# Row sums of a softmax taken off TensorE: additions on GpSimd and VectorE in place of a column of ones, in a hybrid attention step on one NeuronCore

## The chip, the cores and the metric

One core of one Trainium2 chip runs the whole program. The metric is the device time of one execution in microseconds. The profile is one more execution of the same program, taken by the hardware profiler; its own time is 710.37 us.

## The reference, cut to what matters

One layer of a diffusion backbone: 1024 latent tokens and 128 prompt tokens, width 1024, all in float32. A combined projection feeds two groups of heads, mixer A (every latent token sees 128 cached and 1024 latent keys) and mixer B (a window of 128 each way, the cached keys and a sink logit). Both have 8 query heads and 2 key heads of 64. Their gated outputs go through one output projection. Mixer A for a block of 128 queries:

```python
def one_block(qblk):
    s = jnp.einsum('bqkgd,bskd->bkgqs', qblk, k_all).astype(jnp.float32) * (d ** -0.5)
    p = jax.nn.softmax(s, axis=-1).astype(v_all.dtype)
    return jnp.einsum('bkgqs,bskd->bqkgd', p, v_all)
...
def merge_out(o_a, g_a, o_b, g_b, w_out):
    return jnp.concatenate([o_a * jax.nn.silu(g_a), o_b * jax.nn.silu(g_b)], axis=-1) @ w_out
```

The change is about the softmax's denominator in mixer A and about how the values are multiplied.

## The kernel before, in words

To keep float32 accuracy, every operand of a product is split into a high part in TensorE's fp32r type and a low part, the rest. A product is then three: high by high, low by high, high by low. The first 300 us make the projections and are not touched.

After that the kernel works through units. A unit (t, m, g) is one block of 128 tokens t, one mixer m (0 is A, 1 is B) and one key head g, that is four query heads of 128 queries, 512 columns. The order is A, B, A, B for each of the eight latent blocks, so units with even numbers from 0 to 30 are A and odd ones B; then come four short units for the prompt. A latent A unit has nine blocks of 128 keys, a B unit four (three at the two ends). Each block is one *slot* of a written-out schedule (lines 1287 to 1344): in slot s the program issues the scores of block s, the work that is due in that slot (`due`, `later(n, f)`: n slots later), some output products (`outq`, at `OUTRATE` 2.5 a slot), and the products with the values of block s - 3 (`LAG`). Each engine executes its instructions in exactly this order (`in_order`), so an instruction that waits holds up all that stand behind it on its engine.

A block of A (function `scores`): TensorE makes `st` (keys by queries, lines 1179 and 1180; the second product adds minus the row maximum, which lies in rows 64 to 67 of `qb`), ScalarE makes `pe` = exp (L1182) and its high part `ph` (L1186), GpSimd the low part `pl` = pe - ph (L1190; block 4 is VectorE's, L1188). Three slots later `values` adds three products to the bank `pv`: `v_hi` by `ph` (L1200), `v_lo` by `ph` (L1202, 64 columns wide), `v_hi` by `pl` (L1203). For A, `v_hi` holds the values' high part beside 64 columns of ones, so rows 64 to 127 of `pv` are the softmax's row sums, already spread over 64 rows. At a unit's end (`END_AT`) ScalarE makes the sums' inverse by Ln and Exp (L1214, L1215), VectorE multiplies (L1224), GpSimd multiplies by the gate `sgl` (L1226), and the result is split into `ogh` and `ogl` (L1236, L1238) for the output products (L1271).

A B unit has its weights made ahead, while the A unit before it runs: TensorE makes `sn` (L994, L995), VectorE adds the mask and takes the maximum into `nm` (L998), ScalarE makes the exponentials `pen` (L984). Its four slots then only transpose `pen` (L1174), take the high part (L1175) and the low part (VectorE, L1176). B's row sums come as a by-product of L984; they are turned, written to DRAM and read back as rows spread over partitions (L1046 to L1057), and GpSimd multiplies `sgl` by them (L1042).

The next A unit's row maxima are made over A and B slots: products `pmx` (L939), VectorE's maxima `mx` (L940), `m_nat` (L949), a transpose `ptm` (L956) and `qb` (VectorE, L957).

PSUM has eight banks: two called A (pmx, sn, ptm, pti and others), two B (st), two C (pv), D and E (output products).

Of the kernel before, what the change touches and what calls it, by code (L numbers as in the profile page):

```python
# [34 lines left out]
KS = (0, 1, 4, 5, 2, 3, 6, 7)  # L35
PL_DVE = (4,)
LAG = 3
# [9 lines left out]
PH_DVE = 0  # L47
MX_NEXT = (-8, -7, -6, -5, -4, 4, 5, 5, 7, 7, 8, 8)
# [24 lines left out]
NOG = 5  # L73
PES = 3
GATE_LATE = 2
END_AT = (1, 4, 6, 9)
EDGE_END = (1, 3, 6, 9)
PROMPT_END = (2, 4, 5, 7)
# [40 lines left out]
def hybrid_step(ctx, tc, x_prompt, x_sample, cache_k_a, cache_v_a, cache_k_b, cache_v_b,  # L119
# [11 lines left out]
    gate_row = dram.tile([2, D], F32, name="gate_row")  # L131
    r_dram = [dram.tile([4, P], F32, name=f"rd{i}") for i in range(2 * NL)]

# [3 lines left out]
    def later(n, f):  # L137

        agenda.setdefault(now[0] + n, []).append(f)
# [625 lines left out]
    v_hi = kv.tile([P, 2, 20, 2, HD], F32R, name="v_hi")  # L765
    v_lo = kv.tile([P, 20, HD], F32R, name="v_lo")

# [6 lines left out]
    def split_values(src, j):  # L774

        nc.vector.tensor_tensor(v_lo[:, j : j + 2, :], src[:, 0], v_hi[:, 0, j : j + 2, 0, :], op=ALU.subtract)
        nc.vector.tensor_tensor(v_hi[:, 1, j : j + 2, 1, :], src[:, 1], v_hi[:, 1, j : j + 2, 0, :], op=ALU.subtract)

    with tc.tile_pool(name="kt", bufs=2) as kt:
        W_GB.pools[WRAW : WRAW + 2] = [(kt, 2)] * 2  # L780
        sg_tile.append(lambda n: kt.tile([P, 512], F32, tag="kh", name=n))
        for b in range(0, 20, 4):
            later(4 + b // 2, lambda b=b: nc.gpsimd.tensor_scalar(
                v_hi[:, 0, b : b + 4, 1, :], gain4, 0.0, 1.0, op0=ALU.mult, op1=ALU.add))
        ones = ident_r.bitcast(F32)[64:68].unsqueeze(1)
# [116 lines left out]
    qs = ctx.enter_context(tc.tile_pool(name="qs", bufs=2, side="right"))  # L902
    qs.tile([P, 32], F32, name="pad2", bufs=1)
    qp = ctx.enter_context(tc.tile_pool(name="qp", bufs=2, side="right"))
# [17 lines left out]
    def max_items(i):  # L922
# [4 lines left out]
        def item(h, b):  # L927
            if h == 0 and b == 0:
                mxtile[i] = qs.tile([P, 4, 3], F32, tag="mx", name=f"mx{i}", bufs=3)
            mx = mxtile[i]  # L930
            lhs = qtile[i][:, P * h : P * h + P]
            pm = bank("DE"[(h + b) % 2] if i in WIDE_MAX else "A", f"pmx{i}_{h}_{b}")
            if t == 0:
                for h in range(4):
                    hs = slice(P * h, P * h + P)
                    nc.tensor.matmul(pm[:, hs], qtile[i][:, hs], khp[:, g, :], start=True, stop=True)
                nc.vector.tensor_reduce(mx[:, :, 0], pm.rearrange("p (h n) -> p h n", h=4), axis=AX.X, op=ALU.max)
            else:
                nc.tensor.matmul(pm[:, 0:384], lhs, kha[:, g, 3 * b : 3 * b + 3, :], start=True, stop=True)  # L939
                nc.vector.tensor_reduce(mx[:, h, b : b + 1], pm[:, 0:384], axis=AX.X, op=ALU.max)  # L940
# [25 lines left out]
    def weight_items(i):  # L966
# [81 lines left out]
        def put():  # L1048
            iv = spare[0:4, 512 : 512 + P]
            (nc.vector.tensor_copy if i == 1 else nc.scalar.copy)(iv, v["pt"])  # L1050
            nc.sync.dma_start(r_dram[i // 2], iv)

        def rows():
            v["rows"] = spare[:, 512:768].rearrange("p (c n) -> p c n", c=2)
            for s in range(2):
                nc.sync.dma_start(v["rows"][HD * s : HD * s + HD],
                                  r_dram[i // 2].rearrange("(c s) n -> s c n", s=2)[s : s + 1].to_broadcast([HD, 2, P]))  # L1057

# [81 lines left out]
    def blocks(t, m, g):  # L1140

        if t == 0:
            k = (khp[:, g, :], klp[0:68, g, :]) if m == 0 else 0
            return [(k, v_hi[:, m, 18 + g], v_lo[:, 18 + g, :])]
        if m == 0:
            return [((kha[:, g, b, :], kla[:, g, b, :]), v_hi[:, 0, 2 * b + g], v_lo[:, 2 * b + g, :]) for b in range(9)]
# [19 lines left out]
    def scores(i, b, blk):  # L1166
# [13 lines left out]
        nc.tensor.matmul(s, kl, qbtile[i], start=False, stop=True)  # L1180
        pe = w3.tile([P, 512], F32, tag="pe", name=f"pe{i}_{b}", bufs=PES)
        nc.scalar.activation(pe, s, AF.Exp)  # L1182
        if i == 0 and b < PH_DVE:
            nc.vector.tensor_copy(ph, pe)
        else:
            nc.scalar.copy(ph, pe)  # L1186
        if b in PL_DVE:
            later(1, lambda: nc.vector.tensor_tensor(pl, pe, ph, op=ALU.subtract))  # L1188
        else:
            nc.gpsimd.tensor_tensor(pl, pe, ph, op=ALU.subtract)  # L1190
        return ph, pl

    def values(i, b, last, blk, ph, pl):
# [6 lines left out]
        nc.tensor.matmul(pv, two, ph, start=(b == 0), stop=False)  # L1200
        if m == 0:
            nc.tensor.matmul(pv[0:64, :], vl, ph, start=False, stop=False)  # L1202
# [6 lines left out]
        def inverse():  # L1209
            v["rs"] = w2.tile([64, 512], F32, tag="rs", name=f"rs{i}", bufs=1)  # L1210
            if m == 1:
                nc.scalar.copy(v["rs"], pv[64:128, :])
                return
            nc.scalar.activation(v["rs"], pv[64:128, :], AF.Ln)  # L1214
            nc.scalar.activation(v["rs"], v["rs"], AF.Exp, scale=-1.0)  # L1215

        def gated():
# [5 lines left out]
            for s in range(2):  # L1223
                nc.vector.tensor_tensor(of[64 * s : 64 * s + 64], pvv[:, :, s, :], srv[:, :, s, :],  # L1224
                                        op=ALU.add if m else ALU.mult)
            nc.gpsimd.tensor_tensor(of, of, sgl.pop(i), op=ALU.mult)  # L1226
            later(GATE_LATE, lambda: load_gate(i + 2))
            v["of"] = of

        def parts():  # L1230
            while held[0] == NOG:
                outq.pop(0)()
            held[0] += 1
# [5 lines left out]

        ends = (EDGE_END if m == 0 and t in (1, NL) else END_AT) if t else PROMPT_END  # L1240
        for n, f in zip(ends, (inverse, gated, parts)):
# [16 lines left out]
    def out_items(t, g):  # L1258
# [3 lines left out]
        def mm(n, k, p):  # L1262

            if k == KS[0] and p == 0:
                po[n] = bank("DE"[n], f"po{t}_{n}")
            if n == 0 and k == KS[4] and p == 0:
# [8 lines left out]
            if k == KS[-1] and p == 2:  # L1275
# [6 lines left out]

        ks = KS[4 * g : 4 * g + 4]
        return [lambda n=n, k=k, p=p: mm(n, k, p)
                for kk in ((ks[:2], ks[2:]) if last else (ks,)) for n in range(2) for k in kk for p in range(3)]
# [38 lines left out]
    for s in range(len(slots) + LAG + PROMPT_END[3]):  # L1324
# [83 lines left out]
```

## Time and profile before

| what | before |
|---|---|
| runs | 709.97, 710.36, 710.41 us, median 710.36 |
| profiled execution, its own time | 710.37 us |
| its span | 708.4 us |
| instructions | 10641 |
| mean clock of TensorE granted | 0.999 |
| busy PE / DVE / ACT / POOL | 98% / 63% / 59% / 47% of the span |

PE is TensorE's products, PEld its weight loads, DVE VectorE, ACT ScalarE, POOL GpSimd, SP the queue that issues most transfers. A group's row gives line, engine, operation, output and input tiles, shape and count, then busy us and mean ns of one, then the idle time in front of it and what ended it. A row of the timeline gives start and duration in us, then the same names. Matmuls overlap, so a matmul's cost is the distance from its start to the next one's, not its duration.

### The profile page before, as it was taken

The page shows a single profiled execution, that of the slowest core. Times are in us where ns is not written, and L with a number is a line of the kernel's source. Part 1 is how long each engine was busy: PE and PEld are TensorE (multiplying, and loading weights), DVE is VectorE, ACT ScalarE, POOL GpSimd, SP SyncE. Part 2 cuts the span into 40 slices and gives each one's busy share as a digit, 9 for nine tenths or more (in the row PEclk, how much of TensorE's full clock was granted, in tenths as well). Part 3 has the DMA queues.
Part 4 walks back from the last instruction along what each step waited for, and adds up shares of the span by engine and source line. Part 5 has one row for each costly group of instructions (what it writes and reads, how often), then busy time and mean ns, then how long its engine had stood idle before and what let it go on. Part 6 is the DMA issues. An engine that isn't in the chain of part 4 may idle for free.

```text
span 708.4 us, 10641 instructions
## 1 busy us (share of the span) xinstructions
PE 694.0 (98%) x3522; PEld 556.9 (79%) x3522; DVE 446.5 (63%) x995; ACT 414.6 (59%) x834; POOL 334.1 (47%) x349
## 2 busy tenths in 40 slices
PE   6999999999999999999999999999999999999997
PEld 2778988877788889976788788878888888787875
DVE  4555247866677763566667577567676775775563
ACT  5546412421324441179877877787788778877860
POOL 2456024233223330245877655755575547555751
PEclk9999999999999999999999999999999999999999
DMA  9951281238233026423222122122221221212323
GB/s 348 420 186 61 105 303 75 91 113 276 103 134 119 5 72 186 141 70 95 64 93 82 34 82 73 47 81 62 82 70 42 68 89 45 83 52 90 91 75 126
DMA packets 53303, 78.57 MB, mean 111 GB/s; under 512 B 6584, under 2 KB 25464, under 8 KB 52352
## 3 DMA queue, kind: packets, MB, share of 16 engines
q1 hardware_dynamic: 45936, 66.92, 28.9%
q10 hardware_dynamic: 7312, 10.98, 4.1%
q8 instruction: 28, 0.46, 0.3%
q14 instruction: 27, 0.22, 0.1%
HBM read 58.69 MB, written 19.18 MB: 110 GB/s over the span
## 4 chain that ended last, share of the span: by engine, by line
PE 92%; DMA 3%; ACT 2%; issue 1%; DVE 1%; POOL 1%; SPq 0%; ACTq 0%; POOLq 0%; DVEq 0%
PE po L1271 14%; PE pv L1203 7%; PE pv L1200 6%; PE st L1179 5%; PE pmx L939 5%; PE pq L262 5%; PE pq L264 5%; PE pq L263 5%; PE st L1180 5%; PE pv L1202 5%; PE st L1174 4%; PE pg L276 3%; PE pg L272 3%; PE pg L277 3%; PE pk L264 2%; PE pk L262 2%
## 5 line engine op out<-in xcount | busy, mean ns | idle before, releaser
L1190 POOL TENSOR_TENSOR pl<-pe,ph 128x512 fp32r<-128x512 f32 x130 | 167.7, 1292 | 151.2 <-ACT ph L1186 65.7
L940 DVE TENSOR_REDUCE mx<-pmx 128x1 f32<-128x384 f32 x192 | 100.9, 553 | 63.4 <-PE pmx L939 60.9
L1182 ACT ACTIVATE pe<-st 128x512 f32<-128x512 f32 x146 | 86.9, 595 | 29.6 <-PE st L1180 28.9
L1186 ACT CAST ph<-pe 128x512 fp32r<-128x512 f32 x146 | 90.6, 620 | 4.9
L1203 PE MATMUL pv<-pl,v_hi 128*128 128x512 f32 x208 | 82.5, 397 | 0.9 <-POOL pl L1190 0.5
L1200 PE MATMUL pv<-ph,v_hi 128*128 128x512 f32 x208 | 82.4, 396 | 0.0
L1271 PE MATMUL po<-wo,ogh 128*128 128x512 f32 x216 | 73.2, 395 | 0.1
L187 POOL TENSOR_TENSOR rs_q<-ms_q,mhalf 128x8 f32<-128x8 f32 x18 | 34.8, 1933 | 80.9 <-DVE ms_q L185 80.9
L998 DVE CUSTOM_DVE_ANT_0 sn<-sn,mask,nsink 128x512 f32<-128x512 f32 (+1 forms) x64 | 46.4, 725 | 39.1 <-PE sn L995 38.4
L939 PE MATMUL pmx<-kha,qt 128*128 128x384 f32 x192 | 60.4, 364 | 0.9 <-DVE nm L998 0.7
L1179 PE MATMUL st<-qt,kha 128*128 128x512 f32 x144 | 58.1, 403 | 0.7 <-DVE inv L1033 0.5
L1202 PE MATMUL pv<-ph,v_lo 128*64 128x512 f32 x146 | 57.6, 395 | 0.0
L1180 PE MATMUL st<-qb,kla 68*128 68x512 f32 x144 | 57.2, 398 | 0.0
L1203 PEld LDWEIGHTS pv<-pl,v_hi 128*128 128x128 f32 x208 | 39.2, 188 | 18.2 <-POOL pl L1190 1.0
L705 ACT CAST qo0q<-ptq 128x512 fp32r<-128x512 f32 x18 | 10.6, 587 | 65.8 <-PE ptq L702 65.3
L984 ACT ACTIVATE pen<-sn,nm 128x512 f32<-128x512 f32 (+2 forms) x72 | 45.0, 626 | 5.9 <-DVE nm L1011 2.6
L1175 ACT CAST ph<-st 128x512 fp32r<-128x512 f32 x62 | 36.4, 587 | 20.1 <-PE st L1174 18.8
L1271 PEld LDWEIGHTS po<-wo,ogh 128*128 128x128 f32 x216 | 39.9, 188 | 6.8 <-ACT ogh L1236 0.5
L1200 PEld LDWEIGHTS pv<-ph,v_hi 128*128 128x128 f32 x208 | 39.3, 189 | 6.7 <-ACT ph L1175 0.2
L1176 DVE TENSOR_TENSOR pl<-st,ph 128x512 fp32r<-128x512 f32 x62 | 42.6, 689 | 2.8 <-ACT ph L1175 2.2
L1271 PE MATMUL po<-wo,ogl 128*128 128x512 f32 x108 | 42.7, 395 | 0.3 <-POOL ogl L1238 0.3
L939 PEld LDWEIGHTS pmx<-kha,qt 128*128 128x128 f32 x192 | 35.2, 190 | 8.5 <-DVE mx L940 2.9
(230 smaller groups left out, 1687.4 us busy)
## 6 DMA issues: line engine op xcount, KB each, us to landing
qt<-qd SPq DMA_DIRECT2D x72, 128.0 KB, 2.9
wm<-in_w_mod_ss_dram SPq DMA_DIRECT2D x7, 1024.0 KB, 9.4
qd<-qo0q ACTq DMA_DIRECT2D x18, 256.0 KB, 2.5
sgl<-gd SPq DMA_DIRECT2D x36, 128.0 KB
out_dram<-yt SPq DMA_DIRECT2D x17, 256.0 KB, 2.0
xn<-in_x_sample_dram SPq DMA_DIRECT2D x8, 512.0 KB
wg<-in_w_mod_g_dram SPq DMA_DIRECT2D x4, 1024.0 KB, 8.9
wraw<-in_w_out_dram SPq DMA_DIRECT2D x16, 256.0 KB, 5.0
```

What stands on the lines that cost most here:

```text
L262: nc.tensor.matmul(out, h_at(0, i, k, tok), w.hi[k], start=(k == 0), stop=False)
L939: nc.tensor.matmul(pm[:, 0:384], lhs, kha[:, g, 3 * b : 3 * b + 3, :], start=True, stop=True)
L940: nc.vector.tensor_reduce(mx[:, h, b : b + 1], pm[:, 0:384], axis=AX.X, op=ALU.max)
L1179: nc.tensor.matmul(s, kh, qtile[i], start=True, stop=False)
L1180: nc.tensor.matmul(s, kl, qbtile[i], start=False, stop=True)
L1182: nc.scalar.activation(pe, s, AF.Exp)
L1186: nc.scalar.copy(ph, pe)
L1190: nc.gpsimd.tensor_tensor(pl, pe, ph, op=ALU.subtract)
L1200: nc.tensor.matmul(pv, two, ph, start=(b == 0), stop=False)
L1202: nc.tensor.matmul(pv[0:64, :], vl, ph, start=False, stop=False)
L1203: nc.tensor.matmul(pv, two, pl, start=False, stop=last)
L1271: nc.tensor.matmul(po[n], a, wo_parts[KT * n + k][lo], start=(k == KS[0] and p == 0), stop=(k == KS[-1] and p == 2))
```

## The change

For the latent units of mixer A, the ones beside the values give way to the values' low part, so that one product makes the high and the low part's share and L1202 falls away for them (144 of 146). The two halves of `pv` are added at the end, as mixer B's already are. The prompt's two A units keep the ones.

The row sums are now made from `pe` itself. Block 0's `pe` lies in PSUM, in bank E, as the accumulator `acc`; its low part moves to VectorE and block 4's to GpSimd. Of the other eight blocks GpSimd adds two and two (L1196 in the new file) one slot after the even one, and VectorE adds each pair to `acc` (L1207) three slots after the even block's scores, for block 8 two slots after them, into the tile `accs`. Then TensorE transposes `accs` (`pts`, L1216), VectorE sums over the keys and inverts (L1220, L1221), TensorE turns the four columns (`pta`, L1225), ScalarE copies them (L1227), SP writes them to DRAM and reads them back as rows (L1228, L1232), and GpSimd multiplies `sgl` by the rows (L1236). Only then the gate product (L1291) can run. For the last A unit an fp32 product with ones (`ptw`, L1240) and three activations do this instead.

Since bank E is taken, the output products of blocks 1 to 7 use bank D alone, first all of one half of the columns, then all of the other, with a pause of two slots between them.

```diff
+SUM_AT = (4, 5, 6, 10, 12)
+SUM_END = (1, 2, 10, 11)
...
-MX_AT = (-4, -3, -2, -2, -1, 4, 5, 5, 7, 7, 8, 8)
+MX_AT = (-4, -3, -2, -1, 2, 3, 4, 4, 5, 6, 7, 8)
...
-PES = 3
+PES = 4
...
-        nc.vector.tensor_tensor(v_lo[:, j : j + 2, :], src[:, 0], v_hi[:, 0, j : j + 2, 0, :], op=ALU.subtract)
+        low = v_hi[:, 0, j : j + 2, 1, :] if j < 18 else v_lo
+        nc.vector.tensor_tensor(low, src[:, 0], v_hi[:, 0, j : j + 2, 0, :], op=ALU.subtract)
...
-        pe = w3.tile([P, 512], F32, tag="pe", name=f"pe{i}_{b}", bufs=PES)
+        if t and b == 0:
+            pe = acc[i] = bank("E", f"acc{i}")
+        else:
+            pe = w3.tile([P, 512], F32, tag="pe", name=f"pe{i}_{b}", bufs=PES)
         nc.scalar.activation(pe, s, AF.Exp)
...
-        if b in PL_DVE:
+        if t and b == 0:
             later(1, lambda: nc.vector.tensor_tensor(pl, pe, ph, op=ALU.subtract))
         else:
             nc.gpsimd.tensor_tensor(pl, pe, ph, op=ALU.subtract)
+        if t and b % 2:
+            odd[i] = pe
+        elif t and b:
+            other = odd.pop(i)
+            later(1, lambda: nc.gpsimd.tensor_tensor(pe, other, pe, op=ALU.add))
+            later(2 if b == 8 else 3, lambda: add(i, b, pe))
         return ph, pl
+    def add(i, b, pe):
+        out = acc[i]
+        if b == 8:
+            out = accs[i] = w2.tile([P, 512], F32, tag="accs", name=f"accs{i}", bufs=1)
+        nc.vector.tensor_tensor(out, acc[i], pe, op=ALU.add)
...
+        def sums():
+            pt = v["pt"] = bank("A", f"pts{i}")
+            for h in range(4):
+                nc.tensor.transpose(pt[:, P * h : P * h + P], accs[i][:, P * h : P * h + P], ident_r.bitcast(F32))
+        def divide():
+            v["sum"], v["inv"] = (qs.tile([P, 4], F32, tag=n, name=f"{n}{i}") for n in ("suma", "inva"))
+            nc.vector.tensor_reduce(v["sum"], v["pt"].rearrange("p (h n) -> p h n", h=4), axis=AX.X, op=ALU.add)
+            nc.vector.reciprocal(v["inv"], v["sum"])
...
+        def scale():
+            nc.gpsimd.tensor_tensor(sgl[i], sgl[i], rows, op=ALU.mult)
...
-        if m == 0:
+        if vl is not None:
             nc.tensor.matmul(pv[0:64, :], vl, ph, start=False, stop=False)
```

How this moves instructions shows best where A unit 14 ends and B unit 15 begins. The number behind a tile's name is its unit, the next one its block.

On GpSimd, from block 5 or 6 of A unit 14 to the first low part of the next A unit, before:

```order
L1190 TENSOR_TENSOR pl14_5_5409<-pe14_5_5412,ph14_5_5408 128x512
L1226 TENSOR_TENSOR spare_3293<-spare_3293,sgl13_5177 128x256
L1030 TENSOR_TENSOR sum15_5301<-sum15_5301,ex15_5302 128x4
L1190 TENSOR_TENSOR pl14_6_5435<-pe14_6_5438,ph14_6_5434 128x512
L1190 TENSOR_TENSOR pl14_7_5449<-pe14_7_5452,ph14_7_5448 128x512
L1190 TENSOR_TENSOR pl14_8_5477<-pe14_8_5480,ph14_8_5476 128x512
L1238 TENSOR_TENSOR ogl13_5471<-spare_3293,ogh13_5470 128x256
L1190 TENSOR_TENSOR pl16_0_5585<-pe16_0_5588,ph16_0_5584 128x512
L1190 TENSOR_TENSOR pl16_1_5608<-pe16_1_5611,ph16_1_5607 128x512
```

and now:

```order
L1191 TENSOR_TENSOR pl14_6_5529<-pe14_6_5532,ph14_6_5528 128x512
L1236 TENSOR_TENSOR sgl12_5302<-sgl12_5302,accs12_5304 128x256
L1196 TENSOR_TENSOR pe14_6_5532<-pe14_5_5509,pe14_6_5532 128x512
L1191 TENSOR_TENSOR pl14_7_5548<-pe14_7_5551,ph14_7_5547 128x512
L1291 TENSOR_TENSOR spare_3304<-spare_3304,sgl12_5302 128x256
L1191 TENSOR_TENSOR pl14_8_5571<-pe14_8_5574,ph14_8_5570 128x512
L1304 TENSOR_TENSOR ogl13_5565<-spare_3304,ogh13_5564 128x256
L1196 TENSOR_TENSOR pe14_8_5574<-pe14_7_5551,pe14_8_5574 128x512
L1304 TENSOR_TENSOR ogl12_5589<-spare_3304,ogh12_5588 128x256
L1191 TENSOR_TENSOR pl16_1_5723<-pe16_1_5726,ph16_1_5722 128x512
```

The next A unit's GpSimd work used to follow one gate part (`ogl`); now two additions of pairs (`pe14_6`, `pe14_8`), the product of the gate with the rows (`sgl12`) and the gate product of A unit 12 stand in between, and the unit's last addition follows all its low parts.

On VectorE, from the next A unit's first maxima to B unit 17's first `sn`, before:

```order
L940 TENSOR_REDUCE mx18_5506<-pmx18_0_0_5507 128x1
L1176 TENSOR_TENSOR pl15_0_5500<-st15_0_5498,ph15_0_5499 128x512
L949 TENSOR_REDUCE m_nat0_108<-mx16_5210 128x4
L940 TENSOR_REDUCE mx18_5506<-pmx18_0_1_5529 128x1
L1176 TENSOR_TENSOR pl15_1_5520<-st15_1_5518,ph15_1_5519 128x512
L940 TENSOR_REDUCE mx18_5506<-pmx18_0_2_5544 128x1
L940 TENSOR_REDUCE mx18_5506<-pmx18_1_0_5547 128x1
L957 TENSOR_TENSOR qb16_5526<-ptm16_5556,diag_110 4x512
L1176 TENSOR_TENSOR pl15_2_5538<-st15_2_5536,ph15_2_5537 128x512
L940 TENSOR_REDUCE mx18_5506<-pmx18_1_1_5571 128x1
L1176 TENSOR_TENSOR pl15_3_5565<-st15_3_5563,ph15_3_5564 128x512
L998 ISA sn17_0_5597,nm17_5593<-sn17_0_5597,mask_2934,nsink_105 128x512
```

and now, in two pieces that follow each other:

```order
L1207 TENSOR_TENSOR acc14_5390<-acc14_5390,pe14_6_5532 128x512
L941 TENSOR_REDUCE mx18_5603<-pmx18_0_0_5604 128x1
L1207 TENSOR_TENSOR accs14_5614<-acc14_5390,pe14_8_5574 128x512
L1177 TENSOR_TENSOR pl15_0_5597<-st15_0_5595,ph15_0_5596 128x512
L950 TENSOR_REDUCE m_nat0_124<-mx16_5296 128x4
L941 TENSOR_REDUCE mx18_5603<-pmx18_0_1_5633 128x1
L1177 TENSOR_TENSOR pl15_1_5624<-st15_1_5622,ph15_1_5623 128x512
L941 TENSOR_REDUCE mx18_5603<-pmx18_0_2_5649 128x1
```

```order
L958 TENSOR_TENSOR qb16_5630<-ptm16_5662,diag_126 4x512
L1177 TENSOR_TENSOR pl15_2_5643<-st15_2_5641,ph15_2_5642 128x512
L941 TENSOR_REDUCE mx18_5603<-pmx18_1_0_5676 128x1
L1220 TENSOR_REDUCE suma14_5686<-pts14_5657 128x4
L1221 RECIPROCAL inva14_5687<-suma14_5686 128x4
L1284 TENSOR_TENSOR spare_3304<-pv14_5475,rs14_5666 64x256 x2
L1177 TENSOR_TENSOR pl15_3_5670<-st15_3_5668,ph15_3_5669 128x512
L999 ISA sn17_0_5706,nm17_5702<-sn17_0_5706,mask_2945,nsink_121 128x512
L999 ISA nm17_5702 128x1
```

The additions into `acc14` and `accs14` stand ahead of B's low parts, of `m_nat`, `qb16` and `sn17`; the reduction of the sums, its inverse and the joining of the halves (`spare` from `pv14`) stand ahead of `sn17`, which they did not before.

On TensorE, the same place, from B unit 15's third block, before:

```order
L1174 MATMUL st15_2_5536<-ident_r_99,pen15_5299 128x128 x4
L939 MATMUL pmx18_0_2_5544<-kha_2275,qt18_5397 128x384
L939 MATMUL pmx18_1_0_5547<-kha_2275,qt18_5397 128x384
L1271 MATMUL po4_0_5550<-wo0_0_3012,ogh12_5379 128x512
L1271 MATMUL po4_0_5550<-wo1_0_3013,ogh12_5379 128x512
L1200 MATMUL pv14_5375<-ph14_8_5476,v_hi_2281 128x512
L1202 MATMUL pv14_5375<-ph14_8_5476,v_lo_2282 64x512
L1203 MATMUL pv14_5375<-pl14_8_5477,v_hi_2281 128x512
L956 MATMUL ptm16_5556<-ident_r_99,m_nat0_108 4x128
L1174 MATMUL st15_3_5563<-ident_r_99,pen15_5299 128x128 x4
```

and now:

```order
L1175 MATMUL st15_2_5641<-ident_r_115,pen15_5393 128x128 x4
L940 MATMUL pmx18_0_2_5649<-kha_2291,qt18_5495 128x384
L1342 MATMUL po3_1_5516<-wo0_11_4004,ogh10_5281 128x512
L1342 MATMUL po3_1_5516<-wo1_11_4005,ogh10_5281 128x512
L1342 MATMUL po3_1_5516<-wo0_11_4004,ogl10_5282 128x512
L1260 MATMUL pv14_5475<-ph14_8_5570,v_hi_2297 128x512
L1263 MATMUL pv14_5475<-pl14_8_5571,v_hi_2297 128x512
L1216 MATMUL pts14_5657<-ident_r_115,accs14_5614 128x128 x4
L957 MATMUL ptm16_5662<-ident_r_115,m_nat0_124 4x128
L1175 MATMUL st15_3_5668<-ident_r_115,pen15_5393 128x128 x4
```

The product of `v_lo` is gone, output products have come in, and the transposes of `accs14` (`pts14`) stand ahead of `ptm16` and B's last block.

More of the change, by code (lines that the diff above doesn't have):

```diff
@@ L931, in item @@
             lhs = qtile[i][:, P * h : P * h + P]
-            pm = bank("DE"[(h + b) % 2] if i in WIDE_MAX else "A", f"pmx{i}_{h}_{b}")
+            pm = bank("AD"[i in WIDE_MAX and (h + b) % 2], f"pmx{i}_{h}_{b}")
             if t == 0:
@@ L1238, in parts @@
             later(1, lambda: nc.gpsimd.tensor_tensor(ol, v["of"], oh, op=ALU.subtract))
-        ends = (EDGE_END if m == 0 and t in (1, NL) else END_AT) if t else PROMPT_END
+        if m == 0 and t:
+            ends = LAST_END if i == PROMPT_AT - 2 else SUM_END
+            for n, f in zip(ends, (inverse, gated, gate_of, parts)):
+                later(n, f)
+            return
+        ends = END_AT if t else PROMPT_END
         for n, f in zip(ends, (inverse, gated, parts)):
```

87 lines of the change are left out of this document (61 added, 26 removed).

## The prediction

> **What bounds the kernel now.** I read the page's first part, then busy time by stretch, then the timelines of PE, GpSimd, VectorE and ScalarE over one pair of units. First the head of the page, one stretch of the steady part (busy us of PE, PEld, DVE, ACT, POOL; clock) and the groups that the change touches:
>
> ```profile
> PE 694.0 (98%) x3522; PEld 556.9 (79%) x3522; DVE 446.5 (63%) x995; ACT 414.6 (59%) x834; POOL 334.1 (47%) x349
> ```
> ```profile
> 400.00:460.00 60.00, 60.00 (x293) 48.33 (x293) 39.72 (x84) 46.62 (x93) 37.01 (x40) 1.00 0.22 65
> ```
> ```profile
> L1190 POOL TENSOR_TENSOR pl<-pe,ph 128x512 fp32r<-128x512 f32 x130 | 167.7, 1292 | 151.2 <-ACT ph L1186 65.7 <-DVE nm L998 63.7 <-POOL pl L1190 11.2
> L1202 PE MATMUL pv<-ph,v_lo 128*64 128x512 f32 x146 | 57.6, 395 | 0.0
> ```
>
> PE is the bound: never idle, clock 1.00, while GpSimd is busy for 37 us of 60 and VectorE for 40. What a matmul costs is its start-to-start distance, since matmuls overlap. PE in an A unit's end and a B unit's start:
>
> ```profile
> 410.30 0.27 PE L1046 MATMUL pti<-ident_r,inv 128*4 128x128 f32 x1
> 410.41 0.60 PE L1174 MATMUL st<-ident_r,pen 128*128 128x128 f32 x4
> 410.77 0.42 PE L939 MATMUL pmx<-kha,qt 128*128 128x384 f32 x1
> 411.02 0.39 PE L1200 MATMUL pv<-ph,v_hi 128*128 128x512 f32 x1
> 411.25 0.40 PE L1202 MATMUL pv<-ph,v_lo 128*64 128x512 f32 x1
> 411.49 0.40 PE L1203 MATMUL pv<-pl,v_hi 128*128 128x512 f32 x1
> ```
>
> A 128x512 matmul costs 0.235 us, four transposes 0.36, a transpose of a few rows 0.11. GpSimd over the same repeating pair of units (one A, one B):
>
> ```profile
> 443.39 1.30 POOL L1190 TENSOR_TENSOR pl<-pe,ph 128x512 fp32r<-128x512 f32 x1 [0.70 <-ACT ph L1186]
> 444.64 0.74 POOL L1042 TENSOR_TENSOR sgl<-sgl,spare 128x256 f32<-128x256 f32 x1
> 445.33 0.74 POOL L1226 TENSOR_TENSOR spare<-spare,sgl 128x256 f32<-128x256 f32 x1
> 446.03 1.29 POOL L1190 TENSOR_TENSOR pl<-pe,ph 128x512 fp32r<-128x512 f32 x1
> 449.54 0.20 POOL L1016 TENSOR_TENSOR ex<-nm,sink 128x4 f32<-128x4 f32 x1
> 449.69 0.74 POOL L1238 TENSOR_TENSOR ogl<-spare,ogh 128x256 fp32r<-128x256 f32 x1
> ...
> 458.41 0.74 POOL L1238 TENSOR_TENSOR ogl<-spare,ogh 128x256 fp32r<-128x256 f32 x1
> 465.26 1.29 POOL L1190 TENSOR_TENSOR pl<-pe,ph 128x512 fp32r<-128x512 f32 x1 [6.10 <-DVE nm L998]
> 467.25 1.30 POOL L1190 TENSOR_TENSOR pl<-pe,ph 128x512 fp32r<-128x512 f32 x1 [0.70 <-ACT ph L1186]
> ```
>
> Block 1's low part starts at 443.39 and again at 467.25: a pair takes 23.86 us. Back to back, a 128x512 operation costs 1.25 us, a 128x256 one 0.70, a small one 0.15. Between the pairs GpSimd idles 6.1 us: that is the room into which the change puts its additions.
>
> **What PE gains.** Per latent A unit nine products L1202 go: 9 x 0.235 = 2.1 us. Added: four transposes and one small, 0.47. Net 1.64, so PE alone would take 22.2 us per pair, about 25 us less over 15 pairs. ScalarE loses one of two activations of the inverse and gains a small copy; it was busy 46.6 of 60 and stays off the path.
>
> **What GpSimd gets.** From one unit's block 1 to its last addition (order above), GpSimd has eight low parts and four additions (12 x 1.25 = 15.0), five 128x256 operations (two gate products, the new product with the rows, one of B's rows, one low part of the output: 3.5), two small (0.3): 18.8 us in a row. No addition of this shape is in the trace; the nearest row is L1190, same engine, shape and two SBUF inputs, so I take its 1.25. Bounds: 1.20 to 1.32, the spread of that line's spacing and durations by my estimate, 0.6 us per pair each way. The Trainium skill ("GPSIMD Engine Reference", Performance versus the Vector engine) advises against plain elementwise work there and gives 4497 ns for a two-input addition of 2048 elements; by that, as an estimate, 512 take 1.12 us, the pair would be 1.5 us shorter and the whole some 23 us less. The trace has 1.25 for a subtraction, and that decides.
>
> In sum GpSimd has 20.3 us of work per pair, less than 22.2, and by capacity alone it would fit. It doesn't fit in order, because of what hangs on the last addition.
>
> **The wait that is added.** VectorE's accs operation waits for GpSimd's last addition. Behind it on VectorE stand B's first low part, m_nat, the key maxima, qb (the bias row that the next A unit's first scores need), and only then sn of block 0, whose nm lets ScalarE go on to the next unit's block 1. Before, no such step on VectorE waited for GpSimd. VectorE's and ScalarE's rows for these steps:
>
> ```profile
> 461.63 0.68 DVE L957 TENSOR_TENSOR qb<-ptm,diag 4x512 fp32r<-4x512 f32 x1 [0.36 <-PE ptm L956]
> 462.34 0.69 DVE L1176 TENSOR_TENSOR pl<-st,ph 128x512 fp32r<-128x512 f32 x1
> 462.95 0.55 DVE L940 TENSOR_REDUCE mx<-pmx 128x1 f32<-128x384 f32 x1
> 463.47 0.69 DVE L1176 TENSOR_TENSOR pl<-st,ph 128x512 fp32r<-128x512 f32 x1
> 464.40 0.76 DVE L998 CUSTOM_DVE_ANT_0 sn<-sn,mask,nsink 128x512 f32<-128x512 f32 x1 [0.24 <-PE sn L995]
> 465.08 0.14 DVE L998 DVE_READ_ACCUMULATOR2_ANT nm<- 128x1 f32 x1
> 466.93 0.84 DVE L1224 TENSOR_TENSOR spare<-pv,rs 64x256 f32<-64x256 f32 x2
> 469.97 0.69 DVE L1280 TENSOR_TENSOR yt<-po,yt 128x512 f32<-128x512 f32 x1
> ```
> ```profile
> 465.25 0.69 ACT L984 ACTIVATE pen<-sn,nm 128x512 f32<-128x512 f32 x1
> ...
> 465.93 0.59 ACT L1182 ACTIVATE pe<-st 128x512 f32<-128x512 f32 x1
> 466.56 0.62 ACT L1186 CAST ph<-pe 128x512 fp32r<-128x512 f32 x1
> ```
>
> From the last addition: accs 0.7 (as L1280: one input in PSUM), three low parts of B and a fourth 4 x 0.61, three maxima 3 x 0.52, qb 0.7, the reduction to suma 0.65 (128x512 from PSUM, as L1280), two small ones 0.3, the pair into spare 0.84, sn with nm 0.82: 8.0. In between PE holds qb up: B's third block needs a bank that only the first low part frees, and behind it stand a maximum, output products, two values, the sums' transposes and m_nat's (0.36 + 0.25 + 3 x 0.235 + 0.47 + 0.36 + 0.27 = 2.4, less 1.8 of VectorE's own work beside them): 0.6 more. ScalarE from nm (465.22) over the exponential of B, the exponential and the copy of block 1 to GpSimd's block 1 (467.25): 2.0. GpSimd also waits some 0.35 for block 4, since ScalarE does four exponentials of B between blocks 0 and 4. Sum 18.8 + 8.0 + 0.6 + 2.0 + 0.35 = 29.8 us per pair, against 23.9: **6.0 us more**, PE idle for 7.6 of them. The terms are links of one closed chain, each waiting for the one before, so nothing runs beside them.
>
> **The other edits.** They cost nothing as long as that chain is the longest. The rows by DRAM (put, two gets, on SP):
>
> ```profile
> qt<-qd SPq DMA_DIRECT2D x72, 128.0 KB, 2.9
> ```
>
> Put and get take some 3 us each by this row; the get starts about 5 us after nm, the product on GpSimd is its thirteenth step, 12 us behind block 1. Without this cover up to 3 us per pair. On SP the get stands behind query loads and the result's store, which wait for VectorE; 5 us are spare there too. One half of the output in bank D at a time: PE skips output work for two slots while VectorE empties it (2 x 0.69); PE idles anyway, uncovered 1.4 us every second pair. A's gate product moves from 4 slots behind its last values to 10, its output parts from 6 to 11; the output products that read them still come two slots later, and would otherwise cost PE time that it idles anyway. Fewer fills of ones on GpSimd and a fourth pe buffer lie off the path.
>
> **The sum.** Where the chain starts, turns and ends:
>
> ```profile
> 305.86 5.03 POOL L1190 TENSOR_TENSOR pl<-pe,ph 128x512 fp32r<-128x512 f32 x4 [8.41 <-ACT ph L1186]
> ```
> ```profile
> 371.79 1.30 POOL L1190 TENSOR_TENSOR pl<-pe,ph 128x512 fp32r<-128x512 f32 x1 [0.70 <-ACT ph L1186]
> ```
> ```profile
> 655.81 1.29 POOL L1190 TENSOR_TENSOR pl<-pe,ph 128x512 fp32r<-128x512 f32 x1 [0.42 <-ACT ph L1186]
> ```
> ```profile
> 672.13 0.39 PE L1203 MATMUL pv<-pl,v_hi 128*128 128x512 f32 x1
> ```
>
> - First three pairs, block 1 at 307.1 (305.86 + 1.25) to 371.79, 64.7 us. The same chain: 22.5 (no 128x256 work yet, three B blocks), 28.3 (one weight split more), 32.3 (two more) = 83.1: +18.4.
> - Twelve pairs to 655.81, 284.0 us: 11 x 29.8 + 27.0 (three B blocks) = 354.8: +70.8.
> - The end: the last value product started 16.3 us after block 1. Now accs stands ahead of it (18.8 + 0.35 + 0.7), then the product with ones (about 0.9, an estimate: an fp32 product counted as four of 0.235), 0.36 + 0.4 + 0.7 of other PE work: 22.2, +5.9. Behind it stand 111 output products instead of 100: 11 x 0.235 = 2.6. +8.5.
>
> Together 97.7. The profiled execution took 710.37 us (span 708.4 and 2.0 around it), the median of the runs is 710.36. Forecast **808 us**. Low end: no hold-up of qb, no wait for block 4 (0.95 x 15 = 14), additions at 1.20 (9), a shorter end (8), and some links shorter by 0.5 (7): 770. High end: additions at 1.32 (11), a wait of 1 us per pair for rows or banks (15): 834.
>
> **Rivals.**
>
> *Slower by less.* Part of the return lies beside GpSimd's work in a way I missed: 730 to 770. For it: waits are inferred; against: each link is an instruction's place in its engine. 0.05.
>
> *Faster: GpSimd's wide operation is cheaper than its row.* Place: the 12 wide operations between block 1 and accs. The chain is 12 x w + 3.8 + 11.0 with w the cost of one; it falls under today's 23.9 where w is under 0.76, and under PE's 22.2 where w is under 0.62. For it: GpSimd's spans are rough, the page says, and an addition isn't a subtraction. Against: spacing, not spans, gave 1.25, and four in 5.03 us above agree. Time 710.4 - 25 = 686. 0.05, and 0.02 for w near 0.76, where gain and loss cancel: 710.
>
> *Slower still: the clock.* Here PE idles, as in two stretches of today's trace:
>
> ```profile
> 300.00:340.00 40.00, 37.88 (x179) 28.20 (x178) 26.49 (x62) 33.71 (x70) 22.16 (x23) 1.00 0.26 80
> 700.00:708.40 8.40, 3.59 (x16) 2.63 (x14) 2.61 (x5) 0.00 (x0) 0.72 (x1) 0.90 0.28 95
> ```
>
> With PE idle for 4.8 us of 8.4 the clock fell to 0.90 on average; with short gaps it stayed at 1.00. If it halved ahead of accs, the 2.1 us of PE work that hold qb up would double: 2.1 x 15 = 32 us, 840. The Trainium skill ("TensorE: Matmul & The Clock Gate", Part 1: The HAM clock gate) halves the clock after an idle window of about 3.4 us; the trace agrees in that only the long stretch lost clock. PE's gaps would be 2 to 3 us, so 0.06.
>
> *The loop as forecast*: 0.82. Less than 0.2%, 1.4 us, can't be told from no change. Faster 0.05, same 0.02, slower 0.93. The range leaves out 0.18 of the cases.
>
> **What would show it.** Right: block 1 of A units every 29 to 31 us; VectorE's accs waits for GpSimd's last addition, some 3 us or more each time; PE idle a quarter of the steady part; no L1202 but in the prompt's units. Wrong: pairs of 22 to 24 us, additions under 1 us, or VectorE at accs with the addition long done.

## The result, and the profile after

The changed kernel takes 842.09 us, the median of 4 runs (841.97 to 844.4), against 710.16 us: a ratio of 1.1866, 95% interval 1.1844 to 1.1887. Slower was forecast, and the chain that makes it so, but not by how much: 842 lies above the range's end of 834. The profiled execution took 844.4 us, with a span of 842.6; all profile numbers below are from it, so sums of them lie some 2 us above the median's.

From the page of the changed kernel, the first part and three groups (count | busy us, mean ns of one | idle us just before them, and what ended it); then one stretch of the steady part (busy us of PE, PEld, DVE, ACT, POOL; granted clock; DMA share; GB/s):

```profile
PE 728.8 (86%) x3455; PEld 567.3 (67%) x3455; DVE 496.9 (59%) x1089; ACT 404.7 (48%) x836; POOL 419.3 (50%) x425
L1191 POOL TENSOR_TENSOR pl<-pe,ph 128x512 fp32r<-128x512 f32 x130 | 166.8, 1284 | 189.8 <-ACT ph L1187 145.7
L1196 POOL TENSOR_TENSOR pe<-pe,pe 128x512 f32<-128x512 f32 x64 | 82.0, 1281 | 1.4
L1207 DVE TENSOR_TENSOR accs<-acc,pe 128x512 f32<-128x512 f32 x16 | 11.1, 692 | 66.1 <-POOL pe L1196 66.1
```
```profile
400.00:460.00 60.00, 48.74 (x208) 37.32 (x207) 35.97 (x75) 31.94 (x66) 36.29 (x38) 0.89 0.20 58
```

TensorE was 98% busy and is 86% busy; in the stretch it works for 48.7 us of 60, and its clock is 0.89 where it was 1.00. VectorE's last addition (accs) stood idle for 66.1 us over 16 units, always for GpSimd. GpSimd stood idle for 189.8 us before its low parts, 145.7 of them for ScalarE's copy. This reads as a closed chain: each waits for the one before it.

The time per pair is read from one small operation, GpSimd's ex behind block 4, in the fourth and the fifteenth pair:

```profile
404.78 0.21 POOL L1017 TENSOR_TENSOR ex<-nm,sink 128x4 f32<-128x4 f32 x1
755.16 0.20 POOL L1017 TENSOR_TENSOR ex<-nm,sink 128x4 f32<-128x4 f32 x1
```

350.38 us for 11 pairs are 31.85 us each. The same marks of the kernel before stand at 377.95 and 639.90: 23.81 us. One pair of the changed kernel, GpSimd from block 1 to the last addition and to the next block 1:

```profile
429.65 1.28 POOL L1191 TENSOR_TENSOR pl<-pe,ph 128x512 fp32r<-128x512 f32 x1 [12.35 <-ACT ph L1187]
...
447.61 1.25 POOL L1196 TENSOR_TENSOR pe<-pe,pe 128x512 f32<-128x512 f32 x1
...
461.33 1.29 POOL L1191 TENSOR_TENSOR pl<-pe,ph 128x512 fp32r<-128x512 f32 x1 [11.79 <-ACT ph L1187]
```

and VectorE between the two:

```profile
448.89 0.69 DVE L1207 TENSOR_TENSOR accs<-acc,pe 128x512 f32<-128x512 f32 x1 [3.88 <-POOL pe L1196]
449.50 0.68 DVE L1177 TENSOR_TENSOR pl<-st,ph 128x512 fp32r<-128x512 f32 x1
...
451.77 0.56 DVE L941 TENSOR_REDUCE mx<-pmx 128x1 f32<-128x384 f32 x1 [0.46 <-PE pmx L940]
454.44 0.68 DVE L958 TENSOR_TENSOR qb<-ptm,diag 4x512 fp32r<-4x512 f32 x1 [2.11 <-PE ptm L957]
455.15 0.69 DVE L1177 TENSOR_TENSOR pl<-st,ph 128x512 fp32r<-128x512 f32 x1
...
458.49 0.75 DVE L999 CUSTOM_DVE_ANT_0 sn<-sn,mask,nsink 128x512 f32<-128x512 f32 x1
459.16 0.14 DVE L999 DVE_READ_ACCUMULATOR2_ANT nm<- 128x1 f32 x1
```

From GpSimd's block 1 (429.65) to accs (448.89) 19.24 us, where 19.15 were forecast; from accs to the end of nm (459.30) 10.41, forecast 8.6; from there to the next block 1 (461.33) 2.03, forecast 2.0. The sum is 31.68. The surplus is in VectorE's stretch, 1.8 us, and most of it at one row: VectorE stood idle for 2.11 us ahead of qb, where I had 0.6. What held it up is TensorE:

```profile
445.58 0.40 PE L1263 MATMUL pv<-pl,v_hi 128*128 128x512 f32 x1
450.33 1.09 PE L1175 MATMUL st<-ident_r,pen 128*128 128x128 f32 x4 [4.35 <-DVE m_nat L950]
451.07 0.67 PE L940 MATMUL pmx<-kha,qt 128*128 128x384 f32 x1
451.54 1.05 PE L1342 MATMUL po<-wo,ogh 128*128 128x512 f32 x2
...
453.95 0.46 PE L957 MATMUL ptm<-ident_r,m_nat 128*4 128x128 f32 x1
454.20 0.80 PE L1175 MATMUL st<-ident_r,pen 128*128 128x128 f32 x4
...
455.69 0.63 PE L1342 MATMUL po<-wo,ogh 128*128 128x512 f32 x2
```

TensorE stands still for 4.35 us, until VectorE's first low part of B frees a bank (the releaser named is the small operation behind it). After that four transposes take 1.09 us where they take 0.60, and two output products 1.05 where two take 0.63: the matmuls start 0.42 us apart (their pitch), not 0.235. Four microseconds later the pitch of 0.235 is back. The transposes, the maximum, the output and value products and the sum's transposes in that stretch are just the ones that stand before qb.

### The profile page after: what moved, and what is told of

Read it like the earlier page. It is cut to its first block, busy times and chain, and to the rows that moved or that the text cites. A ratio compares the mean times of both kernels' runs of the same rounds, so it can differ in the third digit from the quotient of the medians.

```text
span 842.6 us, 10796 instructions
## 1 busy us (share of the span) xinstructions
PE 728.8 (86%) x3455; PEld 567.3 (67%) x3455; DVE 496.9 (59%) x1089; ACT 404.7 (48%) x836; POOL 419.3 (50%) x425
## 4 chain that ended last, share of the span: by engine, by line
PE 57%; POOL 15%; ACT 11%; DVE 9%; issue 5%; DMA 2%; SPq 0%; POOLq 0%; ACTq 0%; DVEq 0%
PE po L1342 8%; POOL pl L1191 8%; ACT pen L985 4%; PE pq L264 4%; PE pq L266 4%; PE pq L265 4%; POOL pe L1196 3%; PE pmx L940 3%; ACT pe L1186 3%; ACT ph L1187 3%; PE st L1175 3%; PE pv L1260 3%; PE pg L278 3%; PE pg L274 3%; PE pv L1263 3%
## 5 line engine op out<-in xcount | busy, mean ns | idle before, releaser
L1191 POOL TENSOR_TENSOR pl<-pe,ph 128x512 fp32r<-128x512 f32 x130 | 166.8, 1284 | 189.8 <-ACT ph L1187 145.7
L1175 PE MATMUL st<-ident_r,pen 128*128 128x128 f32 x248 | 47.0, 323 | 62.1 <-DVE m_nat L950 50.8
L940 PE MATMUL pmx<-kha,qt 128*128 128x384 f32 x192 | 77.5, 411 | 26.2 <-DVE mx L941 16.7
L1186 ACT ACTIVATE pe<-st 128x512 f32<-128x512 f32 x130 | 77.1, 593 | 21.6 <-PE st L1181 20.3
L1175 PEld LDWEIGHTS st<-ident_r,pen 128*128 128x128 f32 x248 | 34.7, 168 | 74.9 <-issue 59.7
L1187 ACT CAST ph<-pe 128x512 fp32r<-128x512 f32 x130 | 80.7, 621 | 4.1
L1196 POOL TENSOR_TENSOR pe<-pe,pe 128x512 f32<-128x512 f32 x64 | 82.0, 1281 | 1.4
L1342 PE MATMUL po<-wo,ogh 128*128 128x512 f32 x216 | 80.7, 431 | 0.5 <-DVE yt L1351 0.5
L1207 DVE TENSOR_TENSOR acc<-acc,pe 128x512 f32<-128x512 f32 x48 | 33.4, 695 | 33.4 <-POOL pe L1196 33.4
L1207 DVE TENSOR_TENSOR accs<-acc,pe 128x512 f32<-128x512 f32 x16 | 11.1, 692 | 66.1 <-POOL pe L1196 66.1
L1342 PEld LDWEIGHTS po<-wo,ogh 128*128 128x128 f32 x216 | 44.9, 212 | 6.8 <-DVE yt L1351 1.4
```

The costliest lines, as they stand in the source:

```text
L1175: nc.tensor.transpose(s[:, P * h : P * h + P], penat[i][:, h, o : o + P], ident_r.bitcast(F32))
L1196: later(1, lambda: nc.gpsimd.tensor_tensor(pe, other, pe, op=ALU.add))
L1342: nc.tensor.matmul(po[n], a, wo_parts[KT * n + k][lo], start=(k == KS[0] and p == 0), stop=(k == KS[-1] and p == 2))
```

## Experiments

Each kernel was run next to the kernel before on the same chip. us per pair is from the marks above (fourth to fifteenth pair).

| kernel | us | ratio to before, 95% | us per pair |
|---|---|---|---|
| before | 710.16 | | 23.81 |
| the change | 842.09 | 1.1844 to 1.1887 | 31.85 |
| one_more | 865.96 | 1.2181 to 1.2218 | 33.10 |
| warm | 831.85 | 1.1704 to 1.1743 | 30.63 |
| warm16 | 823.43 | 1.1578 to 1.1612 | 30.00 |
| ogh_late | 838.13 | 1.1785 to 1.1820 | 31.38 |
| accs_late | 809.69 | 1.1389 to 1.1439 | 29.58 |
| both_late | 824.20 | 1.1593 to 1.1627 | 30.73 |
| accs_ogh_late | 786.10 | 1.1045 to 1.1079 | 27.52 |
| dve_adds | 759.99 | 1.0675 to 1.0727 | 25.92 |
| old_maxima | 751.89 | 1.0579 to 1.0616 | 25.48 |
| dve_adds_ogh | 738.48 | 1.0385 to 1.0420 | 24.46 |
| no_sums | 720.81 | 1.0137 to 1.0168 | 23.81 |
| no_sums_mx | 713.26 | 1.0035 to 1.0068 | 23.05 |

**Is GpSimd's row on the chain?** One wide operation more per unit:

```diff
-            nc.gpsimd.tensor_tensor(pl, pe, ph, op=ALU.subtract)
+            for _ in range(2 if t and b == 5 else 1):
+                nc.gpsimd.tensor_tensor(pl, pe, ph, op=ALU.subtract)
```


> Block 5's low part is written twice by GpSimd (same values), 16 units of A. Theory 1 (closed chain through GpSimd's row, clock halved after the stall): 1.25 us per pair, 15 pairs and the end, +19 to +20, 861 to 863 us. Theory 2 (closed chain, but the missing 34 us are longer steps of VectorE and ScalarE, not the clock): the same, 861. Rival (GpSimd's row is not on the path, VectorE's wait for it hides behind something else): under +5, 842 to 847.

Measured 865.96, 23.9 above the change; 1.25 us more per steady pair, the cost of one operation. GpSimd's row is on the chain with its full length. The operation added is a subtraction; that an addition costs the same is read from the means of the change's rows, 1281 ns and 1284. The total is 3 us above the 863 expected at most; against the change's profiled execution, which lies 2.3 us above its median, the span grows by 21.4 us (864.0 and 842.6).

**Is it the clock?** TensorE gets something harmless to do in its stall, a product that it repeats to the same result:

```diff
-                nc.tensor.matmul(pm[:, 0:384], lhs, ...)
+                for _ in range(11 if i > 4 and (h, b) == (0, 1) else 1):
+                    nc.tensor.matmul(pm[:, 0:384], lhs, ...)
```


> Ten repeats of one key-maximum product (same result, about 1.9 us at full clock) fill part of TensorE's stall of 4.35 us before B's third block; nothing else changes. Theory 1 (the clock halves after the stall and slows what holds up qb): stall under 2.5 us, no matmul at 0.42 us after it, 1.5 to 2.1 us less per pair, 810 to 820 us. Theory 2 (the clock costs nothing on the path): 842 within 4, the pitch of 0.42 after the stall may go or stay. If the repeats themselves lie on the path: 860.

Measured 831.85: 10 us less, where 22 to 32 were expected. The pairs alternate. TensorE's rows behind the stall in two pairs in a row:

```profile
447.82 1.09 PE L1176 MATMUL st<-ident_r,pen 128*128 128x128 f32 x4 [2.62 <-DVE m_nat L951]
449.02 1.05 PE L1343 MATMUL po<-wo,ogh 128*128 128x512 f32 x2
...
479.20 0.63 PE L1176 MATMUL st<-ident_r,pen 128*128 128x128 f32 x4 [2.18 <-DVE m_nat L951]
479.84 0.63 PE L1343 MATMUL po<-wo,ogh 128*128 128x512 f32 x2
```

After a stall of 2.62 us the transposes take 1.09 and two products 1.05; after one of 2.18 they take 0.63 and 0.63. The pairs with the longer stall take 31.3 us, the others 30.1. So with 16 repeats (the 11 in the diff becomes 17):

> As warm, with 16 repeats of the key-maximum product instead of 10 (about 1.1 us more of the stall filled). In warm every second pair still had a stall of 2.6 us with products at 0.43 us behind it and took 31.3 us, the others a stall of 2.2 us, none slowed, and 30.1 us. Theory 1 (the clock, lowered after a stall above some 2.2 to 2.6 us, is what a pair takes above 30.1): all pairs at 30.1, 822 to 827 us. Theory 2 (the alternation is of the output's steps, not of the clock): 832 within 2. If the repeats come onto the path: over 833.

Measured 823.43. The steady stalls are now 1.13 to 1.61 us, no product behind them is slowed, and the pairs take 30.2 and 29.9 us in turn, 30.0 in the mean: the forecast had 29.8. VectorE's stretch from accs to the end of nm is 8.55 us here (445.00 to 453.55), where the forecast had 8.6 and the change has 10.41. TensorE's work from the third block's transposes to the end of ptm takes 2.22 us (446.44 to 448.66), in the change 4.08 (450.33 to 454.41): the difference of 1.86 is the surplus. More work for TensorE made the kernel 18.7 us faster, so the clock's share is shown, and of warm's alternation of 1.2 us all but 0.3 was the clock's.

**Which returns are there besides?** A return is a way by which a late result of GpSimd comes back to hold up GpSimd's own next block 1; together with GpSimd's row up to that result it closes a ring. VectorE's last addition is put right ahead of the next A unit's first exponential, and the sum's steps behind it go two slots later:

```diff
-SUM_AT = (4, 5, 6, 10, 12)
+SUM_AT = (6, 7, 8, 10, 12)
...
         if t and b == 0:
+            while held_add:
+                held_add.pop(0)()
             pe = acc[i] = bank("E", f"acc{i}")
...
-            later(2 if b == 8 else 3, lambda: add(i, b, pe))
+            if b == 8:
+                end_at[i] = now[0]
+            if b in (8,) and i < PROMPT_AT - 2:
+                held_add.append(lambda: add(i, b, pe))
+            else:
+                later(2 if b == 8 else 3, lambda: add(i, b, pe))
...
-            later(n - 2, f)
+            later(end_at[i] + n - now[0], f)
```


> VectorE's last addition is put right ahead of the next A unit's first score block, behind qb and B's low parts; the sum's steps follow two slots later, the row get and its product stay. Theory 1: the ring through the last addition opens, and the next longest is the one through block 6's addition, still ahead of B's low parts: 14.2 us on GpSimd and 11.3 back, 25.5 us per pair, stall too short for the clock: 746 us (735 to 765). Theory 2: the same ring but 2 us more per pair, 776. Rival (GpSimd's amount of work sets the time): 842 within 5.

Measured 809.69, 29.58 us per pair: a third of what the opened ring should have given. There is a second return, which I had not priced. GpSimd's and ScalarE's rows (accs_late):

```profile
419.92 1.28 POOL L1193 TENSOR_TENSOR pl<-pe,ph 128x512 fp32r<-128x512 f32 x1 [7.15 <-ACT ph L1189]
...
437.98 0.74 POOL L1298 TENSOR_TENSOR spare<-spare,sgl 128x256 f32<-128x256 f32 x1
```
```profile
438.75 0.40 ACT L1309 CAST ogh<-spare 128x256 fp32r<-128x256 f32 x1 [2.79 <-POOL spare L1298]
439.06 0.58 ACT L1176 CAST ph<-st 128x512 fp32r<-128x512 f32 x1
```
```profile
449.47 1.29 POOL L1193 TENSOR_TENSOR pl<-pe,ph 128x512 fp32r<-128x512 f32 x1 [6.91 <-ACT ph L1189]
```

A's gate product ends on GpSimd at 438.72, 18.8 us behind block 1, and ScalarE's copy of it, 2.79 us idle, stands ahead of B's copies. From there it goes over B's low parts to the next block 1: 10.75 us, in sum 29.55. In both_late block 6's addition is put at the same late place (the 8 in the diff becomes 6 and 8):

> As accs_late, and block 6's addition is moved to the same place, so that VectorE waits for GpSimd only there. Theory 1: ring of GpSimd's 19.2 us, two additions' rest 0.7, sn 0.8, ScalarE 2.0 to 2.6: 22.7 to 23.3 us per pair, TensorE's own 22.2 near it: 711 us (700 to 722). Theory 2: the same without the clock's share, 711 to 725. Rival (amount of work on GpSimd, or a wait for rows or banks): over 780.

Measured 824.20, 14.5 slower than accs_late, against all that was expected. VectorE's rows:

```profile
447.28 0.69 DVE L1214 TENSOR_TENSOR acc<-acc,pe 128x512 f32<-128x512 f32 x1
448.06 0.69 DVE L1214 TENSOR_TENSOR accs<-acc,pe 128x512 f32<-128x512 f32 x1
```

Block 6's addition was moved off a return that was not the longest and put onto the one that was, ahead of accs and sn: 0.78 us between the two starts, of 1.15 more per pair. This is read from the rows, and the other 0.37 us were not traced.

So ScalarE's copy (with what reads it) was put two slots later in all but the last three A units, alone and together with accs_late:

```diff
             ends = LAST_END if i == PROMPT_AT - 2 else SUM_END
+            if i < PROMPT_AT - 6:
+                ends = ends[:3] + (13,)
...
-            later(ends[3], lambda: outq.extend(out_items(t, g)))
+            later(ends[3] + 2 * (0 < i < PROMPT_AT - 6), lambda: outq.extend(out_items(t, g)))
```


> ScalarE's copy of A's gated values (high part) and what reads it come two slots later, behind B's first two copies; VectorE's last addition stays where the change put it. Theory 1 (several returns from GpSimd beside each other, the one by VectorE's last addition the longest): 842 within 4. Rival (ScalarE's wait for GpSimd's gate product is the return that sets the pair): 31.9 falls toward 29, 800 to 815.

> Last addition late, as in accs_late (809.7 us, 29.6 us per pair), and ScalarE's copy of A's gated values two slots later. Theory 1: in accs_late the second return, by ScalarE's copy (waits of 2.9 to 4.5 us), set the pair; without it the ring through block 6's addition is next, 25.5 us and some 3 us in which GpSimd waits for A's first blocks: 775 to 795 us. Rival (what is left in accs_late is the banks that the sum's transposes now take from B's scores): 810 within 5.

Measured 838.13 alone, 4 less than the change, and 786.10 together. Alone each edit gives 4 and 32, both together 56: they are returns beside each other, and the longer one hides the other. What was left in accs_ogh_late was not taken apart further.

**Without VectorE waiting for the last additions.** VectorE adds blocks 5 to 8 itself, two more operations there and two less on GpSimd; with and without the late copy:

```diff
-        if t and b % 2:
+        if t and b > 4:
+            later(2, lambda: add(i, b, pe))
+        elif t and b % 2:
             odd[i] = pe
...
```


> Blocks 5 to 8 are added by VectorE one by one, without GpSimd (two wide operations less there, two more of 0.61 us on VectorE); places as in the change. Theory 1: VectorE waits for GpSimd only at block 4's addition, the return by ScalarE's copy of A's gated values is left: 14.7 us on GpSimd and about 10 back, 24.7 us per pair, 734 us (725 to 750). Rival (two wide operations of 1.25 us less is all): 31.9 - 2.5, 805. Rival (VectorE's work becomes the bound): 21 us per pair are under TensorE's 22, so not over 735.

> As dve_adds, and ScalarE's copy of A's gated values two slots later. Theory 1: no return from GpSimd is left over 22.2 us, TensorE sets the pair again, 22.2 to 23.2 us: 698 to 712. Rival (the return by ScalarE doesn't count): as dve_adds within 4.

Measured 759.99 and 738.48. Both are far below the rival's 805, which counted GpSimd's work alone, and the copy's wait was worth 21.5 us once it was the longest return. But the first is 26 us over what Theory 1 gave, and the second 26 over the end of its range. A stretch of dve_adds_ogh:

```profile
460.00:520.00 60.00, 57.83 (x282) 45.38 (x281) 50.15 (x104) 43.59 (x90) 44.20 (x49) 1.00 0.25 76
```

TensorE is busy for 57.8 of 60 us at full clock, and a pair still takes 24.46 us, not 22.2. In dve_adds_ogh the key maxima were put back where they were before:

```diff
-MX_AT = (-4, -3, -2, -1, 2, 3, 4, 4, 5, 6, 7, 8)
+MX_AT = (-4, -3, -2, -2, -1, 4, 5, 5, 7, 7, 8, 8)
```


> As dve_adds_ogh (738.5 us, 24.5 us per pair), with the key maxima at the slots of the kernel before (none in A's slots 0 to 3, two in slot -2). If the maxima in A's slots 2 and 3, where ScalarE sets the pace, hold TensorE up: 23.5 us per pair, 722 to 730. If the sum's transposes then meet more maxima in bank A: 740 to 750. Neither: 738 within 3.

Measured 751.89, slower by 13: here the new places are the better ones.

**Is TensorE's gain there at all?** All additions on both engines and the steps behind them are taken out, so A's values stay without their denominator; no_sums_mx has the old places of the maxima besides:

```diff
-        if t and b % 2:
-            odd[i] = pe
-        elif t and b:
-            other = odd.pop(i)
-            later(1, lambda: nc.gpsimd.tensor_tensor(pe, other, pe, op=ALU.add))
-            later(2 if b == 8 else 3, lambda: add(i, b, pe))
```


> A's row sums are left out altogether: no additions on GpSimd and VectorE, no transposes, reduction, rows by DRAM or product with them (A's values stay unscaled). What is left is the values' high and low part in one product and the other edits. Theory 1 (what TensorE gains is there, and the sums' waits alone cost the time): 21.7 to 22.2 us per pair, 676 to 692 us. Rival (the other edits, gate product late, one half of the output at a time, places of the key maxima, cost time by themselves): 705 or more.

> As no_sums (A's row sums left out, 720.8 us, 23.8 us per pair), with the key maxima at the slots of the kernel before, none in A's slots 0 to 3. In no_sums TensorE has 2 us less to do per pair and stands for 2 us in A's first slots, mostly before key maxima that wait for a bank from ScalarE. If the places of the maxima cost that: 22.2 us per pair, 698 to 705 us. If ScalarE's row of three activations per slot sets the pace there, whatever TensorE is given: 718 to 723.

Measured 720.81 and 713.26: even with sums that cost nothing the kernel is not faster than before, but 1.5% and 0.5% slower, small differences whose intervals leave out 1. The rival was right. TensorE in A's first slots, and ScalarE there (no_sums):

```profile
427.71 0.40 PE L1181 MATMUL st<-qb,kla 68*128 68x512 f32 x1
428.51 1.00 PE L940 MATMUL pmx<-kha,qt 128*128 128x384 f32 x2 [0.40 <-DVE mx L941]
429.36 0.40 PE L1254 MATMUL pv<-ph,v_hi 128*128 128x512 f32 x1
```
```profile
427.72 0.62 ACT L1187 CAST ph<-pe 128x512 fp32r<-128x512 f32 x1
428.25 0.68 ACT L985 ACTIVATE pen<-sn,nm 128x512 f32<-128x512 f32 x1
428.83 0.19 ACT L985 ACTIVATION_READ_ACCUMULATOR pen<-sn,nm 128x1 f32 x1
428.92 0.58 ACT L1186 ACTIVATE pe<-st 128x512 f32<-128x512 f32 x1
```

From a score product to the next two maxima 0.80 us, and from these to the value product 0.85, more than twice what their pitch would make. ScalarE goes from one activation to the next without a gap. Such pauses have to come to some 2 us per pair: the nine products are gone, 2.1 us, and the pair is as long as before. The old places of the maxima get 0.76 of it back (with the sums in, above, they cost time); that ScalarE's row holds the rest is read from these rows, not shown. In no_sums_mx the 11 steady pairs save 8.4 us, and the stretch up to the fourth pair (384.19 against 377.95) and that behind the last mark (52.3 against 47.2) give back 6.2 and 5.1. Which of the other edits does that was not tried.

## Why the prediction was wrong

**The chain: right.** GpSimd's 18.8 and 0.35, its place in the ring, and ScalarE's 2.0 came out within 0.1 us. one_more gives the slope, warm16 the period at full clock (30.0 for 29.8), accs_late and dve_adds that it opens where it was said to close.

**The step that failed** is the clock rival's "PE's gaps would be 2 to 3 us, so 0.06", by which the sum got no term for the clock. It takes the 7.6 us of idle time as several gaps. The order of instructions shows otherwise: TensorE's next work waits for B's first low part, which stands behind accs, so TensorE's idle time ahead of it is one piece, from its last product until accs and the low part are done, 3.9 or 4.35 us in turn. The clock was halved behind every one of them, and 2.62 us were enough in warm, so a gap of 2 to 3 us would not have been safe either. The rival gave 840 and its mechanism is what happened: the ring is longer by 1.85 us per pair (31.85 - 30.00), 18.7 us in all between the medians of the change and warm16. For TensorE's work that is doubled the rival had 2.1 us, the sum 2.4 for the same work; warm16 has 2.22. That 840 lies so near 842 is partly luck: the rival had nothing for the end, where the table below has 5.9 us more than forecast.

**The sum by its three stretches**, forecast and measured, from block 1's starts:

| stretch | forecast | measured |
|---|---|---|
| first three pairs | +18.4 | +25.5 |
| twelve pairs | +70.8 | +94.3 |
| the end | +8.5 | +14.4 |

The 23.5 us of the second row are 12 times 1.85 and 1.3 more. For the other two the cause is read, not tested. In the first pairs stalls of 3.16 and 5.61 us are followed by slowed transposes; at the end the product with ones comes behind a stall of 3.75 us and takes 1.97 us for its two parts, where I had 0.9:

```profile
354.46 1.08 PE L1175 MATMUL st<-ident_r,pen 128*128 128x128 f32 x4 [3.16 <-DVE pl L1177]
...
386.84 1.08 PE L1175 MATMUL st<-ident_r,pen 128*128 128x128 f32 x4 [5.61 <-DVE m_nat L950]
```
```profile
794.60 0.33 PE L1008 MATMUL sn<-khp,qt 128*128 128x128 f32 x1 [3.75 <-ACT spare L1051]
...
797.37 1.97 PE L1240 MATMUL ptw<-accs,v_hi 128*64 128x512 f32 x2 [0.17 <-DVE qb L958]
```

**"They cost nothing as long as that chain is the longest"**, said of the other edits, fits the one of them that was tried behind the chain (ogh_late: 4 us), but I gave no price for the later gate product as a return of its own. It is the second longest, 29.6 us per pair, and a kernel with the first one mended runs into it.

**"PE alone would take 22.2 us per pair"** failed as the time to which a pair can fall, unseen behind the longer chain. Leaving out products shortens a pair only where TensorE sets the pace; no_sums shows 23.8, and there it is ScalarE and the maxima's banks that seem to set the pace of A's first slots. The rival "faster", 686 us, was out of reach: with no additions at all the kernel takes 713 to 721.

No version here beats the kernel before. The best that computes the whole result is dve_adds_ogh, 738.48.

## What to carry to other kernels

Where an engine in the middle of a loop gets a wait for a slower one, follow every return from the slow engine to its own next start, not only the longest: opening one shows the next, and an operation moved off a shorter return can land on the longest. Work out how long TensorE will stand still in one piece, since a long stall can cost a second time in slowed products behind it. And before pricing what TensorE saves, check in the stretch where the products go whether TensorE is the one that others wait for.

## What the runs showed of the hardware

In the steady part a stall of TensorE of 2.17 to 2.19 us left the pitch as it was in 6 of 6 cases (warm), 2.62 to 2.65 us halved the clock in 5 of 5, and 3.9 to 4.36 us in 11 of 11 (the change); there the clock came back 3.0 to 5.9 us after the stall's end. The length of the stall does not decide alone. In accs_late stalls of one length went both ways, once of five with the slow pitch:

```profile
440.51 0.63 PE L1175 MATMUL st<-ident_r,pen 128*128 128x128 f32 x4 [1.56 <-DVE m_nat L950]
...
499.92 1.08 PE L1175 MATMUL st<-ident_r,pen 128*128 128x128 f32 x4 [1.56 <-DVE m_nat L950]
```

The clock that the traces record shows what decides. In the change and its twelve variants, from 300 us on, it is halved for one, two or three steps of 3.41 us (the last halving, cut off by the end, apart), and the halvings of a run start a whole number of such steps apart. What counts is for how much of one such step TensorE is idle. In warm the longer stall lies mostly in one step: from 444.15 to 447.56 us TensorE works for 1.05 us of 3.41, and from 447.56 to 450.97 the clock is 0.50. The shorter one falls across two, with 2.14 us of work from 474.87 to 478.28 and 2.49 from there to 481.69, and the clock stays at 1.00. Warm's steady halvings lie 61.44 us apart, two pairs and 18 steps, so each kind of stall always meets its step at the same place, and those 6 and 5 cases say little about length by itself. Over these thirteen kernels all 94 full-clock steps with more than 56.4% idle were followed by a halved one and none of the 1519 with less than 42.7%; of the 79 between, 32 were. The ends of matmuls are modelled, so the border may be sharper than that.

The Trainium skill ("TensorE: Matmul & The Clock Gate", Part 1: The HAM clock gate) has the clock halved after at least one idle window of about 3.4 us, and the window runs freely. The steps of 3.41 us and the two outcomes of one stall agree with a free window. That steps with 1.05 and 1.68 us of work (warm, and accs_late from 496.12 to 499.53) were enough does not agree with a window that has to be idle from end to end, and there the measurement decides. Here a stall of 1.56 us in one piece slowed the products behind it once, and one of 3.9 us or more did so each time.
